# Seven block products in place of eight for 35 of 132 pairs of chunks in a decoder layer's feed-forward

## The chip, the cores and the metric

The kernel runs on one core of a Trainium2 chip. The metric is the device time of one execution in microseconds (us), lower is better. Engines are named as in the profile: PE (TensorE, matmuls), DVE (VectorE), ACT (ScalarE), POOL (GpSimd), SP (SyncE, here a queue that issues loads).

## What is computed

One decoder layer on 256 tokens of width 2048, in float32: two attention branches (gated DeltaNet and block-sparse attention), a gated merge, and a dense feed-forward. The change touches the last part:

```python
h = h + jnp.einsum('btd,de->bte', mix, w_out[l])
u = _rmsnorm(h, norm_ffn_w[l])
hid = jax.nn.silu(jnp.einsum('btd,df->btf', u, w_ffn_gate[l])) * jnp.einsum('btd,df->btf', u, w_ffn_up[l])
h = h + jnp.einsum('btf,fd->btd', hid, w_ffn_down[l])
```

The feed-forward is 5632 wide.

## The kernel before

Each matmul operand is split into a high part (float32r) and a remainder, and a product of two operands is three matmuls: high by high, high by remainder, remainder by high. Activations are split once and stay in SBUF (`uT`, the normalised input, and `hid`, the hidden layer, whose buffers are `low` and `high`). Weights stream from DRAM in 503 *units* of 128 x 1024 (512 KB), in the order of use. For each unit SP issues a load into `wraw` (7 buffers), ACT copies it to `whi` (L65), and DVE subtracts to `wlo` (L66); `whi` and `wlo` have 4 buffers each. I call the copy and the subtraction of one unit a *split*. `Weights.get` starts the splits of the next two units ahead; the fourth buffer is free only when PE has done with the unit four before.

A token-major job, `tm_job`, makes 512 output columns for both token tiles (n = 0, 1). One unit holds two *chunks* of 128 rows by 512 columns, so a unit is 2 chunks x 2 token tiles x 3 = 12 matmuls of 128 x 512 (L193 to L195), accumulating in 2 PSUM banks. The pool `mm` has two buffers of two banks each, the pool `aux` four of one bank. The feed-forward is 11 rounds c of a gate job and an up job, 8 units each. After a round, 8 transposes (L205) turn the 512 new hidden columns, and ACT and DVE split them (L860, L861). The down projection is 4 jobs j of 22 units; each ends with an addition of `h` on DVE and a store of the result. The last job finishes token tile 0 four chunks early.

Work beside the matmuls is queued in `late` and `chains`, and `tick()`, called after each unit, issues the next step. The tile framework orders the instructions of each engine; each engine then works through its own queue strictly in that order, so what waits at the head holds up all behind it.

Of the kernel before, what the change touches and what calls it, by code (L numbers as in the profile page):

```python
# [16 lines left out]
P = 128  # L17
# [19 lines left out]


class Weights:

    def __init__(self, nc, pool, src):
        self.nc, self.pool, self.src = nc, pool, src
        self.n = src.shape[0]
        self.raw, self.parts = {}, {}

    def load(self, u, f=slice(0, 1024)):
# [5 lines left out]

    def split(self, u, by_parts=False):
        if u in self.parts or u >= self.n:
            return
        self.load(u)
# [3 lines left out]
        self.parts[u] = (hi, lo)  # L62
# [7 lines left out]
        part(slice(0, 1024))  # L70

    def get(self, u):
        for k in range(u, u + RAW - 1):
            self.load(k)
        for k in range(u, u + SPLIT_AHEAD):
            self.split(k)
        return self.parts.pop(u)


@with_exitstack  # L80
def layer(ctx: ExitStack, tc: tile.TileContext, xT, xtok, params, consts, relt, w_bd, w, out):
# [91 lines left out]

    def tm_job(act, nk, last=0):

        get = act if callable(act) else lambda kc: act[:, kc]
        if last:
            ps = [aux.tile([P, 512], F32, name="ps", tag="aux") for _ in range(NT)]
        else:
            both = mm.tile([P, NT, 512], F32, name="ps", tag="mm")  # L180
            ps = [both[:, n] for n in range(NT)]
        order = [(kc, n) for kc in range(nk - last) for n in range(NT)]
        order += [(kc, n) for n in range(NT) for kc in range(nk - last, nk)]
        units = {}
        for kc, n in order:
            if kc // 2 not in units:
                units[kc // 2] = W.get(cursor[0])
                cursor[0] += 1
            hi, lo = units[kc // 2]
            sl = slice((kc % 2) * 512, (kc % 2) * 512 + 512)  # L190
            ah = get(kc)[:, n * P:(n + 1) * P]
            al = get(kc)[:, T + n * P:T + (n + 1) * P]
            nc.tensor.matmul(ps[n], ah, hi[:, sl], start=kc == 0, stop=False)  # L193
            nc.tensor.matmul(ps[n], ah, lo[:, sl], start=False, stop=False)  # L194
            nc.tensor.matmul(ps[n], al, hi[:, sl], start=False, stop=kc == nk - 1)  # L195
            if n == NT - 1 and kc % 2 == 1:
                tick()
        return ps

    def turn(src, evict):  # L200

        def steps():
            p = aux.tile([P, 4, P], F32, name="pT", tag="aux")
            for i in range(4):
                nc.tensor.transpose(p[:, i], src[:, i * P:(i + 1) * P], ident)  # L205
            evict(p)
        late.append(steps)

    ident = small("ident", [P])
    aT = acts.tile([P, KM, 512], F32R, name="aT", tag="actA")  # L210
    xrow = acts.tile([P, NT, DM], F32, name="xrow", tag="actB")
    with tc.tile_pool(name="xin", bufs=4) as xin:
# [17 lines left out]
        def x_part(k0):  # L230
            part = W.split(cursor[0], k0 == 0)
# [569 lines left out]
    for j in range(4):  # L801
        for n, m in gated(gates(), ybt(), "mixb", mdt):
            nc.vector.tensor_add(m, m, mix[j][n])
            turn(m, halved(j, n))


    h = acts.tile([P, NT, DM], F32, name="h", tag="actB")
    uT = acts.tile([P, KM, 512], F32R, name="uT", tag="actA")
    hss = small("hss", [NT, 4])

    def weighted(j, n):
        def evict(p):
            for i in range(4):
# [7 lines left out]
    for j in range(4):  # L821
# [35 lines left out]
    def parted(c, n):
        def evict(p):
            hi = hid(4 * c, 4)[:, :, n * P:(n + 1) * P]
            nc.scalar.copy(hi, p)  # L860
            nc.vector.tensor_sub(hid(4 * c, 4)[:, :, T + n * P:T + (n + 1) * P], p, hi.bitcast(F32))  # L861
        return evict

    for c in range(KF // 4):
        pg = tm_job(uT, KM)
        if c == 0:
            drain()
        gs = []
        for n in range(NT):
            g = fft("fg")  # L870
            nc.scalar.activation(g, pg[n], AF.Tanh, scale=r2h[:, n:n + 1])
            nc.vector.scalar_tensor_tensor(g, g, 1.0, pg[n], op0=ALU.add, op1=ALU.mult)
            gs.append(g)
        pu = tm_job(uT, KM)
        for n in range(NT):
            nc.vector.scalar_tensor_tensor(gs[n], pu[n], r2q[:, n:n + 1], gs[n], op0=ALU.mult, op1=ALU.mult)
            turn(gs[n], parted(c, n))
# [100 lines left out]
```

## Time and profile before

| | us |
|---|---|
| median of 3 runs (lowest, highest) | 1483.71 (1483.56, 1485.71) |
| the profiled execution's own time | 1483.21 |
| its span, first to last instruction | 1481.3 |
| PE busy in the span | 1473.0 |
| DVE busy | 867.4 |
| ACT busy | 677.8 |
| POOL busy | 31.8 |

Busy time of PE is the sum over matmuls whose ends are modelled; waits are read from the views of waits and of the timeline.

### The profile page before, as it was taken

Reading aid. Unit: us, or ns where it says so; the run is one execution under the profiler, and the core shown is the slowest. Engines: PE = TensorE matmul, PEld = TensorE weight load, DVE = VectorE, ACT = ScalarE, POOL = GpSimd, SP = SyncE. Lnnn points to the kernel's source line nnn. Section 1 sums busy time; section 2 is a strip of 40 time slices with the busy share of each in tenths; the row PEclk is TensorE's granted clock in tenths of the full one; section 3 lists DMA queues with packets and bytes.
Section 4 is the critical chain, followed back from the end, with each engine's and each line's share of the span. In section 5 each row is a group of like instructions: output and inputs, shape, how many; then the busy total and the mean of one; then the engine's idle time right before and its main releaser. Section 6 shows DMA issues by size and latency. Waiting matters only on the chain.

```text
span 1481.3 us, 18784 instructions
## 1 busy us (share of the span) xinstructions
PE 1473.0 (99%) x7182; PEld 1230.7 (83%) x7182; DVE 867.4 (59%) x1188; ACT 677.8 (46%) x968; POOL 31.8 (2%) x32
## 2 busy tenths in 40 slices
PE   9999999999999999999999999999999999999998
PEld 8888888888888888888888888888888888888887
DVE  6887689776764545555665554555554555444443
ACT  6554446645454444444554444443444443333332
POOL 0010000110000000000000000000000000000000
PEclk9999999999999999999999999999999999999999
DMA  9457545575456666677666666666666666676671
GB/s 376 161 179 195 158 142 174 163 188 164 150 164 181 192 195 188 183 220 220 185 186 188 193 189 193 187 187 190 192 189 193 186 187 190 193 211 204 195 209 61
DMA packets 77449, 277.81 MB, mean 188 GB/s; under 512 B 8752, under 2 KB 9392, under 8 KB 76976
## 3 DMA queue, kind: packets, MB, share of 16 engines
q1 hardware_dynamic: 75888, 272.03, 61.0%
q10 hardware_dynamic: 992, 3.02, 0.9%
q0 software_dynamic: 480, 1.57, 0.3%
q8 instruction: 56, 0.92, 0.2%
q14 instruction: 33, 0.27, 0.0%
HBM read 274.36 MB, written 2.23 MB: 187 GB/s over the span
## 4 chain that ended last, share of the span: by engine, by line
PE 97%; DVE 1%; issue 0%; DMA 0%; ACT 0%; POOL 0%; SPq 0%; DVEq 0%; ACTq 0%
PE ps L193 28%; PE ps L194 28%; PE ps L195 28%; PE ps L166 6%; PE ps L167 3%; PE pT L205 1%; PE pga L456 0%; DVE wlo L66 0%; DMA wraw<-in_w 0%; PE pb L300 0%; PE pX L541 0%; PE pY L534 0%; PE pU L584 0%; PE pO L592 0%; PE ptr L432 0%
## 5 line engine op out<-in xcount | busy, mean ns | idle before, releaser
L66 DVE TENSOR_TENSOR wlo<-wraw,whi 128x1024 fp32r<-128x1024 f32 (+1 forms) x505 | 617.5, 1225 | 507.4 <-ACT whi L65 506.7
L65 ACT CAST whi<-wraw 128x1024 fp32r<-128x1024 f32 (+1 forms) x505 | 530.2, 1051 | 709.3 <-PE ps L195 615.9
L193 PE MATMUL ps<-whi,uT 128*128 128x512 f32 x704 | 274.8, 390 | 0.0
L195 PE MATMUL ps<-whi,uT 128*128 128x512 f32 x704 | 273.9, 389 | 0.0
L194 PE MATMUL ps<-wlo,uT 128*128 128x512 f32 x704 | 273.9, 389 | 0.0
L193 PE MATMUL ps<-whi,aT 128*128 128x512 f32 x512 | 204.5, 399 | 0.0
L194 PE MATMUL ps<-wlo,aT 128*128 128x512 f32 x512 | 200.0, 391 | 0.1
L195 PE MATMUL ps<-whi,aT 128*128 128x512 f32 x512 | 199.8, 390 | 0.0
L195 PEld LDWEIGHTS ps<-whi,uT 128*128 128x128 f32 x704 | 132.2, 188 | 27.4
L194 PEld LDWEIGHTS ps<-wlo,uT 128*128 128x128 f32 x704 | 132.2, 188 | 27.1
L193 PEld LDWEIGHTS ps<-whi,uT 128*128 128x128 f32 x704 | 132.2, 188 | 27.0
L166 PE MATMUL ps<-aT,whi 128*128 128x512 f32 x384 | 136.9, 399 | 1.9 <-DVE aT L237 1.9
L195 PEld LDWEIGHTS ps<-whi,aT 128*128 128x128 f32 x512 | 96.1, 188 | 20.2
L193 PE MATMUL ps<-whi,high 128*128 128x512 f32 x288 | 112.0, 389 | 0.0
L194 PE MATMUL ps<-wlo,high 128*128 128x512 f32 x288 | 112.0, 389 | 0.0
L195 PE MATMUL ps<-whi,high 128*128 128x512 f32 x288 | 112.0, 389 | 0.0
L193 PEld LDWEIGHTS ps<-whi,aT 128*128 128x128 f32 x512 | 96.2, 188 | 18.8
L194 PEld LDWEIGHTS ps<-wlo,aT 128*128 128x128 f32 x512 | 96.3, 188 | 18.6 <-DVE wlo L66 0.4
L167 PE MATMUL ps<-aT,wlo 128*128 128x256 f32 x384 | 107.6, 280 | 0.9 <-DVE wlo L66 0.9
L166 PEld LDWEIGHTS ps<-aT,whi 128*128 128x128 f32 x384 | 72.1, 188 | 18.3 <-DVE aT L237 2.2
L167 PEld LDWEIGHTS ps<-aT,wlo 128*128 128x128 f32 x384 | 72.4, 189 | 1.6 <-DVE wlo L66 1.4
L193 PEld LDWEIGHTS ps<-whi,high 128*128 128x128 f32 x288 | 54.1, 188 | 11.3
(328 smaller groups left out, 1373.1 us busy)
## 6 DMA issues: line engine op xcount, KB each, us to landing
wraw<-in_w SPq DMA_DIRECT2D x503, 512.0 KB, 3.7
xrow<-in_xtok SPq DMA_DIRECT2D x1, 2048.0 KB, 13.6
lb<-dm ACTq DMA_DIRECT2D x2, 1024.0 KB
xr<-in_xtok SPq DMA_DIRECT2D x8, 256.0 KB, 5.3
xc<-in_xT SPq DMA_DIRECT2D x3, 512.0 KB, 7.3
out<-fo POOLq DMA_DIRECT2D x6, 256.0 KB, 3.8
bias<-in_relt SPq DMA_DIRECT2D x4, 256.0 KB, 3.9
xc<-in_xT ACTq DMA_DIRECT2D x2, 256.0 KB, 4.4
```

Source lines behind the costliest of these rows:

```text
L65: self.last_hi = self.nc.scalar.copy(hi[:, f], raw[:, f])
L66: self.last_lo = self.nc.vector.tensor_sub(lo[:, f], raw[:, f], hi[:, f].bitcast(F32))
L166: nc.tensor.matmul(ps[:, j], hi[:, sl], act[:, kc], start=kc == 0, stop=False)
L167: nc.tensor.matmul(ps[:, j, :T], lo[:, sl], act[:, kc, :T], start=False, stop=kc == nk - 1)
L193: nc.tensor.matmul(ps[n], ah, hi[:, sl], start=kc == 0, stop=False)
L194: nc.tensor.matmul(ps[n], ah, lo[:, sl], start=False, stop=False)
L195: nc.tensor.matmul(ps[n], al, hi[:, sl], start=False, stop=kc == nk - 1)
L205: nc.tensor.transpose(p[:, i], src[:, i * P:(i + 1) * P], ident)
```

## The change

Two 512-column jobs become one job of 1024 columns, `super_job`: gate and up of a round together, and two output blocks of the down projection. Its eight block products for a pair of chunks are (2 chunks of k) x (2 token tiles) x (2 halves of the columns). For 35 pairs (2 of 8 in each of the 11 rounds, 5 and 8 of 22 in the two down jobs; 132 pairs in all) these are replaced by seven products of sums of blocks. Four results of the seven pairs collect in the job's own banks (`ps`), and the others in four more banks (`pw`), which are put together once per job.

- **Splits.** A plain pair is two units, split whole. A pair of seven products has four splits: the left half of the first unit (`b11`), the second unit (`b2`), and both units again (`t`) after four subtractions in place on DVE (L96, L97, L99, L100). Its PE work per split is 3, 6, 6 and 6 matmuls.
- **Sums of activations.** `make_sums` forms four sums of blocks on POOL (one 128 x 512 addition and four of 128 x 128), copied on ACT and subtracted on DVE into `usum` (2, for all rounds) or `dsum` (8, for both down jobs). Its temporaries `fsum` have 2 buffers.
- **`after`.** When a job's last pair of seven is done, ACT copies the four `pw` banks into `ft`, and POOL makes four additions of 128 x 512 (eight in a down job, where it also adds `h`).
- **`swiglu`.** DVE adds the job's own banks to `ft`, then makes the gate product from SBUF; 8 transposes follow. Jobs alternate between `mm` and `aux` for `ps`, and the transposes and `pw` take the banks of the other pool, which held the previous job's results.
- **h in DRAM.** `h` is stored to DRAM by four DMAs of POOL's queue after the output projection and loaded again by four.

```diff
+FFN_PAIRS = (3, 5)
+FFN_ORDER = [[0, 1, 2, 4, 6, 3, 5, 7]] + [list(range(KM // 2))] * (DFF // 512 - 1)
+DOWN_PAIRS = (4, 8, 12, 15, 18, 2, 6, 10)
+DOWN_USED = [(4, 8, 12, 15, 18), DOWN_PAIRS]
...
+        left, right = slice(0, 512), slice(512, 1024)
+        part(left if kind == "b11" else slice(0, 1024))
+        if kind == "b11":
+            self.load(u + 1)
+            self.nc.vector.tensor_sub(raw[:, left], raw[:, right], raw[:, left])
+            self.nc.vector.tensor_sub(raw[:, right], self.raw[u + 1][:, left], raw[:, right])
+        if kind == "b2":
+            self.nc.vector.tensor_sub(raw[:, left], raw[:, left], self.raw[u - 1][:, left])
+            self.nc.vector.tensor_sub(raw[:, right], raw[:, right], raw[:, left])
...
+            if seven:
+                todo += [([(("s", 0), (2 * p, 0), 0)], 0),
+                         ([(("m", 1), (sums[p], 3), 0), (("m", 0), (2 * p + 1, 0), 1)], 1),
+                         ([(("s", 1), (sums[p], 0), 0), (("s", 3), (sums[p], 2), 1)], 0),
+                         ([(("s", 2), (sums[p], 1), 0), (("m", 2), (2 * p + 1, 1), 1)], 2)]
+            else:
+                todo += [([(("m", 2 * n + f), (2 * p, n), f) for n in range(NT) for f in range(2)], 1),
+                         ([(("m", 2 * n + 1 - f), (2 * p + 1, n), f) for n in range(NT) for f in range(2)], 1)]
...
+        if spare[0] == "mm":
+            both = mm.tile([P, NT, 512], F32, name="pT", tag="mm")
+            p = [both[:, n].rearrange("p (i t) -> p i t", i=4) for n in range(NT)]
+        else:
+            p = [aux.tile([P, 4, P], F32, name="pT", tag="aux") for _ in range(NT)]
...
+        nc.gpsimd.dma_start(hsave[:, :, fs], h[:, :, fs])
...
+    def make_sums(g, c):
...
+        f = fft("fsum", 2).rearrange("p (k t) -> p k t", k=2)
+        nc.gpsimd.tensor_add(f, c[:, :, :T], c[:, :, T:])
+        a11, a21, a12, a22 = f[:, 0, :P], f[:, 0, P:], f[:, 1, :P], f[:, 1, P:]
+        t = fft("fsum", 2).rearrange("p (k t) -> p k t", k=4)
+        nc.gpsimd.tensor_add(t[:, 0], a21, a22)
+        nc.gpsimd.tensor_sub(t[:, 1], t[:, 0], a11)
+        nc.gpsimd.tensor_sub(t[:, 2], a11, a21)
+        nc.gpsimd.tensor_sub(t[:, 3], a12, t[:, 1])
+        yield
+        nc.scalar.copy(g[:, 0], t)
+        nc.vector.tensor_sub(g[:, 1], t, g[:, 0].bitcast(F32))
+        yield
...
+        t = [fft("ft", 4) for _ in range(4)]
+        for a, b in zip(t, s):
+            nc.scalar.copy(a, b)
+        nc.gpsimd.tensor_add(t[2], t[0], t[2])
+        nc.gpsimd.tensor_add(t[3], t[2], t[3])
+        nc.gpsimd.tensor_add(t[2], t[2], t[1])
+        nc.gpsimd.tensor_add(t[1], t[3], t[1])
...
+    def down_sums():
+        for i, p in enumerate(DOWN_PAIRS):
+            yield from make_sums(dsum[:, i], hid(2 * p, 2))
```

Three places of the instruction order. First DVE in the first half of a round, from the end of a round's matmuls to the subtraction after the transposes (`fg` is the gate product, `pT` the transposed PSUM tile). Before:

```order
L66 TENSOR_TENSOR wlo<-wraw,whi 128x1024 x7
L876 SCALAR_TENSOR_TENSOR fg<-ps,r2q,fg 128x512 x2
L66 TENSOR_TENSOR wlo<-wraw,whi 128x1024 x2
L861 TENSOR_TENSOR low<-pT,low 128x4x128 x2
L66 TENSOR_TENSOR wlo<-wraw,whi 128x1024 x6
```

In the changed kernel, from the last step of `swiglu` through the first pair of seven of round 2:

```order
L88 TENSOR_TENSOR wlo<-wraw,whi 128x1024
L960 TENSOR_TENSOR low<-pT,low 128x4x128
L88 TENSOR_TENSOR wlo<-wraw,whi 128x1024
L960 TENSOR_TENSOR low<-pT,low 128x4x128
L88 TENSOR_TENSOR wlo<-wraw,whi 128x1024 x2
L88 TENSOR_TENSOR wlo<-wraw,whi 128x512
L96 TENSOR_TENSOR wraw<-wraw 128x512
L88 TENSOR_TENSOR wlo<-wraw,whi 128x1024
L97 TENSOR_TENSOR wraw<-wraw 128x512
L99 TENSOR_TENSOR wraw<-wraw 128x512
L100 TENSOR_TENSOR wraw<-wraw 128x512
L88 TENSOR_TENSOR wlo<-wraw,whi 128x1024 x8
```

The two subtractions behind the transposes now stand one behind each `t` split of pair 3 (the first two `L88` rows); the row of 128x512 opens pair 5. Second, PE in round 6, after the fifth unit, with buffer numbers (`pw` 8840 and 8841 are two-bank buffers of `mm`; `pT` 8801 holds the second of them until it is read out):

```order
L299 MATMUL pT_8801<-ident_80,fg_8716 128x128 x4
L283 MATMUL pw_8840<-whi_8783,uT_5835 128x512
...
L283 MATMUL pw_8840<-whi_8836,usum_6659 128x512
L284 MATMUL pw_8840<-wlo_8837,usum_6659 128x512
L285 MATMUL pw_8840<-whi_8836,usum_6659 128x512
L283 MATMUL pw_8841<-whi_8836,usum_6659 128x512
```

Before, all 8 transposes stood in a row; now in even rounds the second four stand after the sixth unit, directly ahead of the pair of seven. Third, DVE in the first down job around its first pair of seven (pair 4). Before, from the round's last subtraction to the end of down job 0:

```order
L861 TENSOR_TENSOR high<-pT,high 128x4x128 x2
L66 TENSOR_TENSOR wlo<-wraw,whi 128x1024 x20
L882 TENSOR_TENSOR fo<-ps,h 128x512 x2
```

In the changed kernel, from the third of the eight sums to the seventh:

```order
L976 TENSOR_TENSOR dsum<-fsum,dsum 128x512
L88 TENSOR_TENSOR wlo<-wraw,whi 128x512
L960 TENSOR_TENSOR high<-pT,high 128x4x128 x2
L96 TENSOR_TENSOR wraw<-wraw 128x512
L976 TENSOR_TENSOR dsum<-fsum,dsum 128x512
L97 TENSOR_TENSOR wraw<-wraw 128x512
L88 TENSOR_TENSOR wlo<-wraw,whi 128x1024
L976 TENSOR_TENSOR dsum<-fsum,dsum 128x512
L99 TENSOR_TENSOR wraw<-wraw 128x512
L100 TENSOR_TENSOR wraw<-wraw 128x512
L88 TENSOR_TENSOR wlo<-wraw,whi 128x1024
L976 TENSOR_TENSOR dsum<-fsum,dsum 128x512
```

All eight sums stand between the splits of units 5 to 15 of down job 0, three of them inside the splits of pair 4.

## Rows read from the trace of the kernel before

**Rows 1.** The page, part 1: busy time by engine; and TensorE's granted clock.
```profile
span 1481.3 us, 18784 instructions
PE 1473.0 (99%) x7182; PEld 1230.7 (83%) x7182; DVE 867.4 (59%) x1188; ACT 677.8 (46%) x968; POOL 31.8 (2%) x32
...
PEclk9999999999999999999999999999999999999999
```

**Rows 2.** The chain that ended last, by engine; then all waits of PE.
```profile
PE 97%; DVE 1%; issue 0%; DMA 0%; ACT 0%; POOL 0%; SPq 0%; DVEq 0%; ACTq 0%
...
PE ps L166 <- DVE aT L237: 1.9, 1, 1.9
PE busy L228 <- DVE ones L116: 1.1, 1, 1.1
PE ps L167 <- DVE wlo L66: 0.9, 1, 0.9
PE pb L300 <- DVE bw L297: 0.5, 1, 0.5
```

**Rows 3.** Timeline in round 5: start, us, engine, line, tile.
```profile
1001.38 0.39 PE L193 MATMUL ps<-whi,uT 128*128 128x512 f32 x1
1001.60 0.39 PE L194 MATMUL ps<-wlo,uT 128*128 128x512 f32 x1
1001.62 1.05 ACT L65 CAST whi<-wraw 128x1024 fp32r<-128x1024 f32 x1 [1.67 <-PE ps L195]
1001.83 0.39 PE L195 MATMUL ps<-whi,uT 128*128 128x512 f32 x1
1002.06 0.39 PE L193 MATMUL ps<-whi,uT 128*128 128x512 f32 x1
...
1002.71 1.23 DVE L66 TENSOR_TENSOR wlo<-wraw,whi 128x1024 fp32r<-128x1024 f32 x1 [1.49 <-ACT whi L65]
```

**Rows 4.** Windows: PE, PEld, DVE, ACT, POOL busy (x), clock, DMA share, GB/s.
```profile
795.80:840.20 44.40, 44.40 (x202) 36.86 (x201) 23.40 (x22) 19.00 (x20) 0.00 (x0) 1.00 0.65 190
```

**Rows 5.** Groups by line and form: DVE, then ACT (busy us, mean ns | idle before).
```profile
L66 DVE TENSOR_TENSOR wlo<-wraw,whi 128x1024 fp32r<-128x1024 f32 x503 | 616.1, 1227 | 502.5 <-ACT whi L65 501.7 <-PE pPT L733 0.6
L876 DVE SCALAR_TENSOR_TENSOR fg<-ps,r2q,fg 128x512 f32<-128x512 f32 x22 | 15.5, 746 | 4.5 <-PE ps L195 4.5
L828 DVE TENSOR_TENSOR h<-ps,xr 128x512 f32<-128x512 f32 x8 | 5.2, 686 | 1.6 <-PE ps L195 1.6
L803 DVE TENSOR_TENSOR mixb<-mixb,mix 128x512 f32<-128x512 f32 x8 | 5.1, 684 | 0.0
L65 ACT CAST whi<-wraw 128x1024 fp32r<-128x1024 f32 x503 | 529.0, 1053 | 707.1 <-PE ps L195 615.9 <-PE ps L166 35.5 <-issue 21.4
L860 ACT CAST high<-pT 128x512 fp32r<-128x512 f32 x18 | 9.6, 586 | 0.0
L65 ACT CAST whi<-wraw 128x512 fp32r<-128x512 f32 x2 | 1.2, 610 | 2.2 <-DMA wraw<-in_w 2.2
```

**Rows 6.** Groups of POOL by line and form.
```profile
L501 POOL TENSOR_TENSOR k<-k,kd 128x512 f32<-128x512 f32 x2 | 2.1, 1040 | 168.6 <-DVE erq L640 121.9 <-DVE bk L445 46.6
L969 POOL MEMSET const-uint8-127<- 128x1 uint8 x1 | 0.1, 103 | 0.0
```

**Rows 7.** Timeline of DVE and POOL, 107 to 112 us.
```profile
107.30 1.49 POOL L452 TENSOR_TENSOR mt<-dec,bk 128x512 f32<-128x512 f32 x1
107.81 2.06 DVE L66 TENSOR_TENSOR wlo<-wraw,whi 128x1024 fp32r<-128x1024 f32 x1
108.86 1.90 POOL L452 TENSOR_TENSOR dec<-dec,rk 128x512 f32<-128x512 f32 x1
...
110.73 1.29 POOL L484 TENSOR_TENSOR ct<-mt,cst 128x512 f32<-128x512 f32 x1
111.34 0.68 DVE L457 TENSOR_TENSOR mt<-mt,pga 128x512 f32<-128x512 f32 x1
```

**Rows 8.** What SP's queue waited for (us, times, longest), and landing of a weight load.
```profile
SPq L53 <- DVE wlo L66: 1071.1, 442, 13.1
...
wraw<-in_w SPq DMA_DIRECT2D x503, 512.0 KB, 3.7
```

**Rows 9.** Timeline at the end: last matmul, addition, store.
```profile
1477.07 0.39 PE L195 MATMUL ps<-whi,high 128*128 128x512 f32 x1
1477.49 0.69 DVE L882 TENSOR_TENSOR fo<-ps,h 128x512 f32<-128x512 f32 x1 [2.03 <-PE ps L195]
1478.22 0.34 ACTq L883 DMA_DIRECT2D out<-fo  x1
```

**Rows 10.** Durations of one subtraction-like line on DVE: min/median/max ns.
```profile
L466 DVE TENSOR_TENSOR mtmp<-mt,cst x4: 910/1344/1789, 107.0 to 301.6; 128x512 f32<-128x512 f32 x4
```

More of the change, by code (lines that the diff above doesn't have):

```diff
@@ L46, in __init__ @@
         self.raw, self.parts = {}, {}
+        jobs = _super_jobs()
+        self.first = self.n - 2 * sum(len(job) for job in jobs)
+        self.plan, self.at = [("all", u) for u in range(self.first)], 0
+        u = self.first
+        for seven in (f for job in jobs for _, f in job):
+            self.plan += [("b11", u), ("b2", u + 1), ("t", u), ("t", u + 1)] if seven else [("all", u), ("all", u + 1)]
+            u += 2
     def load(self, u, f=slice(0, 1024)):
@@ L172, in fm_job, with tm_job @@
         return fm_jobs(act, nk, 1)[0]
[L174 to L189, printed above, removed]
-            sl = slice((kc % 2) * 512, (kc % 2) * 512 + 512)
[L191 to L196, printed above, removed]
+    def tm_job(act, nk):
+        both = mm.tile([P, NT, 512], F32, name="ps", tag="mm")
+        ps = [both[:, n] for n in range(NT)]
+        for kc in range(nk):
+            if kc % 2 == 0:
+                hi, lo = W.get()
+            sl = slice((kc % 2) * 512, (kc % 2) * 512 + 512)
+            for n in range(NT):
+                ah = act[:, kc, n * P:(n + 1) * P]
+                al = act[:, kc, T + n * P:T + (n + 1) * P]
+                nc.tensor.matmul(ps[n], ah, hi[:, sl], start=kc == 0, stop=False)
+                nc.tensor.matmul(ps[n], ah, lo[:, sl], start=False, stop=False)
+                nc.tensor.matmul(ps[n], al, hi[:, sl], start=False, stop=kc == nk - 1)
+            if kc % 2 == 1:
@@ L862, in parted @@
         return evict
-    for c in range(KF // 4):
[L865 to L877, printed above, removed]
@@ new lines, in layer, with ffn_setup, after @@
+    usums = {}
+    def ffn_setup():
+        by_stage.close()
+        later["ff"] = ff = ctx.enter_context(tc.tile_pool(name="ff", bufs=1))
+        later["high"] = ff.tile([P, KF - H, 512], F32R, name="high")
+        yield
+        for p in FFN_PAIRS:
+            usums[p] = ff.tile([P, 2, 4, P], F32R, name="usum", tag="sum", bufs=2)
+            yield from make_sums(usums[p], uT[:, 2 * p:2 * p + 2])
+    parts = []
+    def after(s):
+        t = [fft("ft", 4) for _ in range(4)]
[5 more added lines that the diff above has]
+        nc.gpsimd.tensor_add(t[1], t[3], t[1])
+        parts.append([t[0], t[2], t[3], t[1]])
@@ new lines, in layer @@
+    jobs = _super_jobs()
+    kinds = ("aux", "mm")
+    chains.append(ffn_setup())
+    for c in range(KF // 4):
+        ps = super_job(kinds[c % 2], jobs[c], lambda kc: uT[:, kc], {p: lambda p=p: usums[p] for p in FFN_PAIRS}, after)
+        under_way.append(c)
+        chains.append(swiglu(c, ps, parts.pop()))
+    dsum = acts.tile([P, len(DOWN_PAIRS), 2, 4, P], F32R, name="dsum", tag="actA")
+    def down_sums():
+        for i, p in enumerate(DOWN_PAIRS):
+            yield from make_sums(dsum[:, i], hid(2 * p, 2))
@@ new lines, in down_end, with after_down @@
+    def down_end(j, ps, t, dmas):
+        for i in range(4):
+            n, f = divmod(i, 2)
+            nc.vector.tensor_add(t[i], t[i], ps[i])
+            dmas[i].dma_start(out[:, n, 512 * (2 * j + f):512 * (2 * j + f + 1)], t[i])
+            yield
+        if under_way:
+            under_way.pop()
+    chains.append(down_sums())
+    down = {p: lambda i=i: dsum[:, i] for i, p in enumerate(DOWN_PAIRS)}
+    for j in range(2):
+        hx = [later["ff"].tile([P, NT, 512], F32, name="hx", tag="sum", bufs=2) for _ in range(2)]
+        for f in range(2):
+            nc.gpsimd.dma_start(hx[f], hsave[:, :, 512 * (2 * j + f):512 * (2 * j + f + 1)])
+        def after_down(s):
+            after(s)
+            for i in range(4):
+                n, f = divmod(i, 2)
+                nc.gpsimd.tensor_add(parts[0][i], parts[0][i], hx[f][:, n])
+        ps = super_job(kinds[(KF // 4 + j) % 2], jobs[KF // 4 + j], hid, down, after_down, 2 * j)
+        if j == 0:
+            under_way.append(j)
+            chains.append(down_end(j, ps, parts.pop(), [nc.gpsimd] * 4))
@@ L886, in _bucket @@
+    for _ in down_end(1, ps, parts.pop(), [nc.sync, nc.scalar] * 2):
+        pass
 def _bucket():
```

163 lines of the change are left out of this document (121 added, 42 removed).

## The prediction

> **What bounds the kernel now.** I read the page's busy times and the chain of waits first. PE is busy 1473.0 of 1481.3 us, at a granted clock of 9 tenths or more in every slice [rows 1]; 97% of the chain that ended last is PE's, and all its waits together are 4.4 us, all early in the program [rows 2]. So every matmul taken away is worth its spacing, as long as the others still deliver. The timeline gives that spacing: L193 at 1001.38 and again at 1002.06 with three matmuls between, 0.227 us each; the 0.39 us of a row overlaps the next one's [rows 3]. A unit of 12 is then 2.72 us, and a round of 192 matmuls 43.5 us, with 8 transposes 44.4 us, which is the window of a whole round [rows 4]. In it DVE works 23.4 us and ACT 19.0: there is room, but how much of it lies where it is needed must be asked locally. The copy of a split starts 0.24 us after PE's matmul that opens a unit (1001.62 after 1001.38), since it waits for the `whi` buffer of four units before [rows 3]; then 1.05 us copy, 0.04 us, 1.23 us subtraction: 2.56 us, 5.6 us before PE wants it.
>
> **What is removed.** Each of the 35 pairs loses one block product of three matmuls: 105 x 0.227 = **-23.8 us**. The code and the order ahead of the feed-forward are the same but for names, so nothing moves there. A round becomes 186 matmuls and the transposes, 43.0 us.
>
> **What is added and lies beside PE.** Prices [rows 5]: split 1.053 on ACT and 1.227 on DVE, half a split 0.61 and about 0.69, a DVE operation of 512 from SBUF 0.684, with one input in PSUM 0.686, the scaled one 0.746, an ACT copy from PSUM 0.586. DVE in a round: 12 plain splits 14.7 us; two pairs of seven, each 3.5 splits and four subtractions, 4.3 + 2.7 = 7.0, together 14.1; `swiglu` and the reading of the transposes 7.0 us. That is 35.8 of 43.0 us. ACT: 25 us by the same sum. On average both fit. A pair of seven alone doesn't: 7.0 us of DVE in 21 x 0.227 = 4.76 us of PE, so it lives on the slack of the plain pair beside it (2.45 in 5.44 us), and with four buffers it can only run three splits ahead. The tightest is the second `t`: its copy may start when PE opens `b11`, 3 + 6 + 6 matmuls or 3.4 us ahead; the split takes 2.56 us, and PE wants the remainder only at the unit's second matmul. So 1.07 us are left if DVE is free at that moment. In the second down job plain and seven alternate: DVE 9.5 us in 10.2 us of PE, which holds by the same walk. I cost these at nothing; without that cover each 0.1 us is 3.5 us over 35 pairs.
>
> `after`: four copies (2.4 us of ACT) and four POOL additions at 1.04 us [rows 6] start some 10 us ahead of a round's end, and DVE has only plain splits there: nothing. The stores and loads of `h` add 4 MB to a DMA share of 0.65 [rows 4]: nothing. Weight loads wait for `wlo` of seven units before, 442 times [rows 8]; a pair of seven frees its buffers later, by two splits, but a load lands in 3.7 us [rows 8] and is wanted some 13 us after: nothing. The end keeps its shape, one addition and one store behind the last bank, where now 1477.07 leads to 1478.22 [rows 9].
>
> **What lands on the path.** Three places.
>
> First, round 0 takes its two pairs of seven one behind the other. Count from PE's start of the eighth unit: it opens the first `b11` at 8.2 us, and the second `t` of that pair is copied from 8.4 and subtracted by 10.7. Then DVE has half a split, a subtraction, a split, three subtractions and the next `t`: 0.69 + 0.69 + 1.23 + 2.05 + 1.23 = 5.9, done at 16.6; PE wants it at 15.0 + 0.2. **+1.4 us.**
>
> Second, in even rounds the second four transposes stand after the sixth unit, and `pT` holds the buffer that `pw`'s second half takes. From the round's start: fifth unit ends 13.6, four transposes 0.44, sixth unit to 16.8, transposes, `b11` at 17.2, `b2` 17.9, `t` 19.24; its second product, into that buffer, 19.92. The second `t` is copied 17.44 to 18.5, the transposed tile 18.5 to 19.1; DVE subtracts the `t` until 19.7 and then the tile until 20.4. PE waits 0.5 us, in rounds 2, 4, 6, 8 and 10: **+2.6 us.** In odd rounds all transposes come earlier and both readings are done by 18.3.
>
> Third, the eight sums of the first down job. A sum's four small POOL additions need the buffer that the sum before gives back only after its DVE subtraction, then comes ACT's copy, then DVE's subtraction, which stands at the head of DVE's queue between splits. A 128 x 128 addition on POOL is in no row. The nearest are 1.04 us for 512 columns and 0.10 for one column [rows 6], the bounds; I take 0.34, which is 0.10 and a quarter of the rest. A step is then 4 x 0.34 + 0.59 + 0.68 + 0.15 of handovers = 2.8 us. The first sum ends about 11.0 us after the job's start. If the engines run freely, the fourth ends at 19.6, the fifth at 22.3, and the first `t` of pair 4, behind two more subtractions, at 24.8, just when PE wants it (24.9); the sixth at 25.4 and the second `t` at 26.6, 0.4 us late. But POOL and DVE get in each other's way when both of DVE's inputs are in SBUF: a `wlo` that met a POOL multiplication took 2.06 us instead of 1.23, the next POOL one took 1.90 instead of 1.04, and a DVE operation from PSUM kept its 0.68 beside one [rows 7]. If each step's POOL work first lets pass the splits and subtractions that stand between the sums (1.2, 1.2, 1.3, 1.9 and 2.5 us up to the sixth), the second `t` comes 8 us later still, and the seventh sum adds one or two: 0.4 to 10.5 us. DVE often stands idle at a sum's wait, and POOL goes first then, so I take a value above the middle: **+6 us.**
>
> The Trainium skill, page "SBUF — State Buffer", section "Who interferes with whom", says that a DVE instruction with two SBUF inputs and a GpSimd instruction that reads SBUF share a port held for a whole instruction, so that the second to start is fully blocked, and that one SBUF input doesn't contend. The trace agrees, with the 2.06, 1.90 and 0.68 us above. By the rule alone the third term would be 10.5 us and the time 1473.9 us; without it 0.4 us and 1463.8 us.
>
> **Sum.** -23.8 + 1.4 + 2.6 + 6 = -13.8 us. Against the profiled execution's own 1483.2 us, which is 0.5 us under the median of the three runs, that gives 1469.4 us; I say **1469.4 us**.
>
> **Rivals.** (A) Everything is hidden. For it: PE waited for nothing after the first stage [rows 2], and my three places are built from handovers of a few tenths. Then 1483.2 - 23.8 = 1459.4, with the sums at 0.4 and the other two places as worked out 1463.8. (B) DVE is late in more places. DVE and POOL block each other fully in the sums, 10.5 us, and the cover of 1.07 us in a pair of seven is thin: if 17 of the 35 pairs lose 0.4 us more (6.8 us), 1.4 + 2.6 + 10.5 + 6.8 = 21.3 us come back, 1480.7; with a third of those pairs 1476. (C) Slower. The four subtractions in place cost what L466, a DVE operation of the same size, took beside POOL: 1.34 us, up to 1.79 [rows 10], against 0.68. Four times 0.66 is 2.6 us a pair, 1.07 covered, 1.6 us lost 35 times: 55 us, and 1469.4 + 55 = 1524 us. It decides against the change from 13.8 / 35 = 0.39 us a pair beyond the cover, so from 1.05 us a subtraction. Against it: L466 ran from 107.0 us on, in POOL's stretch [rows 7, 10], POOL is idle where these stand, and L803 with both inputs in SBUF took 0.684 [rows 5]. (D) No change to within 0.2%, or 3 us, which is about what a measurement of this kernel can tell: were POOL's small additions at their upper bound of 1.04 us, the five steps up to the sixth sum would grow by 2.8 us each, 14 us, and 1469.4 would become 1483.4.
>
> **Chances.** The sum's own case, 1463.8 to 1476 us: 0.53. (A) 0.20. (B) 0.18. (D) 0.04. (C) 0.05. Faster by over 0.2% is the first three, 0.91; within 0.2% 0.04; slower 0.05. The range goes from (A)'s better half to (B)'s end: 1460 to 1480 us leaves out the lowest of (A) and all of (C) and (D), under 2 in 10.
>
> **What the profile will show.** PE: 105 fewer matmuls of 512 and still 0.227 us apart. Round 0: a wait of PE for `wlo` of about 1.4 us ahead of the second pair of seven's first `t`. Even rounds: waits of about 0.5 us for DVE's reading of `pT`, none in odd ones. Down job 0: several us of waits for `wlo` between its units 9 and 13, DVE in turn waiting for ACT's `dsum`, ACT for POOL. Down job 1: none. DVE near 36 us in a round of 43. The prediction is wrong low if PE waits in every pair of seven, and wrong high if down job 0 runs through its sums without a gap, or if POOL's small additions take about 0.1 us.

## The result, and the profile after

The changed kernel takes 1473.88 us, the median of 4 runs (1473.38 to 1475.54), against 1483.68 us for the kernel before beside it (4 runs): 0.9933 of the time, 95% interval 0.9915 to 0.9950. That is 9.8 us less, where 14.3 was forecast; 1473.88 lies inside the range of 1460 to 1480 us.

The page of the changed kernel, first the busy times, then PE's share and granted clock in 40 slices of 36.8 us:

```profile
PE 1458.2 (99%) x7077; PEld 1213.5 (82%) x7077; DVE 1078.7 (73%) x1452; ACT 759.9 (52%) x1100; POOL 200.9 (14%) x148
...
PE   9999999999999999999999999999999999899998
...
PEclk9999999999999999999999999999999999899999
```

PE was without a dent before [rows 1]; now its 35th slice has an 8 and the granted clock has one there too. DVE has 211 us more to do in all [rows 1]. The view of PE's waits, whose total was 4.4 us before [rows 2]:

```profile
PE pw L284 <- DVE wlo L88: 3.3, 2, 2.6
...
PE ps L284 <- DVE wlo L88: 1.6, 2, 1.2
PE pw L283 <- ACT whi L87: 1.4, 1, 1.4
...
PE ps L283 <- ACT whi L87: 0.7, 1, 0.7
```

These four rows, all in the changed part, are 7.0 us of waits for splits. 0.7 of it lies in round 0 and 0.4 near the end; the other 5.9 lie in 16 us of down job 0, whose windows show what came with them (busy time and matmuls in brackets of PE, weight loads, DVE, ACT, POOL, then granted clock):

```profile
1227.08:1250.44 23.36, 23.36 (x108) 19.41 (x107) 17.49 (x22) 11.19 (x15) 12.07 (x16) 1.00 0.50 150
1250.44:1266.10 15.66, 9.71 (x24) 6.13 (x23) 10.20 (x10) 5.58 (x8) 13.63 (x15) 0.67 0.29 84
1266.10:1350.00 83.90, 83.90 (x372) 69.45 (x371) 61.76 (x60) 43.30 (x48) 14.00 (x9) 1.00 0.65 209
```

In the middle one PE is busy for 9.71 us only, and at a granted clock of 0.67; ahead of it and behind it PE is busy throughout, at 1.00. PE there, in its timeline (start, duration, idle time before it):

```profile
1250.44 0.39 PE L283 MATMUL ps<-whi,dsum 128*128 128x512 f32 x1
1252.05 0.50 PE L284 MATMUL ps<-wlo,dsum 128*128 128x512 f32 x1 [1.21 <-DVE wlo L88]
...
1253.08 0.40 PE L285 MATMUL ps<-whi,high 128*128 128x512 f32 x1
1254.91 0.51 PE L283 MATMUL pw<-whi,dsum 128*128 128x512 f32 x1 [1.44 <-ACT whi L87]
1258.07 0.80 PE L284 MATMUL pw<-wlo,dsum 128*128 128x512 f32 x1 [2.65 <-DVE wlo L88]
1258.66 0.63 PE L285 MATMUL pw<-whi,dsum 128*128 128x512 f32 x1
1259.08 0.63 PE L283 MATMUL pw<-whi,dsum 128*128 128x512 f32 x1
...
1260.51 0.80 PE L283 MATMUL pw<-whi,dsum 128*128 128x512 f32 x1
1261.95 0.80 PE L284 MATMUL pw<-wlo,dsum 128*128 128x512 f32 x1 [0.65 <-DVE wlo L88]
...
1265.95 0.39 PE L284 MATMUL ps<-wlo,high 128*128 128x512 f32 x1
```

Twenty-two steps lead from 1250.44 to 1265.95, 15.51 us where 22 x 0.227 = 4.99 would do: 10.5 us are lost. Four steps are too long by 1.38, 1.60, 2.93 and 1.21 us, together 7.1. The other 3.4 us are in steps between and behind them, nearly all from 1258.07 to 1265.95, where most matmuls start 0.42 to 0.43 us apart: the 1.2 GHz level, where 0.227 us is the 2.4 GHz one. The Trainium skill, page "TensorE: Matmul & The Clock Gate", section "Back-to-back issue gap", gives 512 columns divided by 1.2 GHz for it, 0.427 us, and the rows agree.

These slow steps are not 3.4 us of a loss of their own. Behind the last of the four waits (1261.95) PE goes on without a wait until it needs the next remainder that stands behind a sum in DVE's queue, that of the unit after the next:

```profile
1265.24 1.23 DVE L976 TENSOR_TENSOR dsum<-fsum,dsum 128x512 fp32r<-128x512 f32 x1 [1.95 <-ACT dsum L975]
1266.40 1.21 DVE L88 TENSOR_TENSOR wlo<-wraw,whi 128x1024 fp32r<-128x1024 f32 x1
...
1268.04 0.39 PE L284 MATMUL ps<-wlo,high 128*128 128x512 f32 x1
```

It is ready at 1267.61, and PE comes for it at 1268.04. At 0.227 us a step the nine steps up to 1265.95 would have taken 2.0 us less, and PE would have come at 1266.1 and waited; and the slow steps ahead of 1261.95 only shortened the wait that ended there. By these rows the lower clock cost some 0.4 us here (an estimate, which takes it that the row of sums doesn't hang on PE's pace), and the row of sums the rest.

What PE waits for there is the row of sums. One step of it, in the timeline of POOL, ACT and DVE:

```profile
1234.99 0.69 DVE L976 TENSOR_TENSOR dsum<-fsum,dsum 128x512 fp32r<-128x512 f32 x1
...
1235.82 0.46 POOL L970 TENSOR_TENSOR fsum<-fsum 128x128 f32<-128x128 f32 x1 [10.01 <-DVE dsum L976]
...
1236.57 1.22 DVE L88 TENSOR_TENSOR wlo<-wraw,whi 128x1024 fp32r<-128x1024 f32 x1 [0.89 <-ACT whi L87]
1236.67 1.45 POOL L971 TENSOR_TENSOR fsum<-fsum 128x128 f32<-128x128 f32 x1
1238.19 0.46 POOL L973 TENSOR_TENSOR fsum<-fsum 128x128 f32<-128x128 f32 x1
1238.69 0.62 ACT L975 CAST dsum<-fsum 128x512 fp32r<-128x512 f32 x1 [2.15 <-POOL fsum L973]
1238.73 1.30 POOL L967 TENSOR_TENSOR fsum<-high 128x512 f32<-128x512 f32 x1
...
1239.34 1.24 DVE L976 TENSOR_TENSOR dsum<-fsum,dsum 128x512 fp32r<-128x512 f32 x1 [1.55 <-ACT dsum L975]
```

A 128 x 128 addition takes POOL 0.46 us, and 1.45 when a `wlo` runs. ACT stands idle at the head of its queue for 2.15 us and DVE for 1.55, each with splits behind that could run. The first sum ends at 1235.68, the sixth at 1260.77: 5.0 us a step in the mean, where 2.8 was forecast for free engines.

The program up to the feed-forward is the same in all kernels here, but its length differs from execution to execution: PE's first matmul on `uT` starts at 748.50 us in the profile of before, at 751.07 in this one, and between 748.3 and 752.1 in the others. So below I compare, beside the medians, the **stretch**: from that matmul's start to the start of the last one. It is 1477.07 - 748.50 = 728.57 us before and 1469.62 - 751.07 = 718.55 us after, 10.0 less. With the 23.8 us removed and nothing lost it would be 704.8, so 13.8 us came back.

### The profile page after: what moved, and what is told of

Read it like the earlier page. It is cut to its first block, busy times and chain, and to the rows that moved or that the text cites. A ratio compares the mean times of both kernels' runs of the same rounds, so it can differ in the third digit from the quotient of the medians.

```text
span 1473.8 us, 19231 instructions
## 1 busy us (share of the span) xinstructions
PE 1458.2 (99%) x7077; PEld 1213.5 (82%) x7077; DVE 1078.7 (73%) x1452; ACT 759.9 (52%) x1100; POOL 200.9 (14%) x148
## 4 chain that ended last, share of the span: by engine, by line
PE 93%; DVE 3%; ACT 1%; issue 1%; POOL 1%; DMA 0%; SPq 0%; DVEq 0%; POOLq 0%; ACTq 0%
PE ps L283 13%; PE ps L284 13%; PE ps L285 13%; PE ps L218 11%; PE ps L219 11%; PE ps L220 11%; PE ps L199 6%; PE ps L200 3%; PE pw L284 2%; PE pw L285 2%; PE pw L283 2%; PE pT L299 1%; DVE wlo L88 1%; ACT whi L87 1%; DVE dsum L976 0%
## 5 line engine op out<-in xcount | busy, mean ns | idle before, releaser
L88 DVE TENSOR_TENSOR wlo<-wraw,whi 128x1024 fp32r<-128x1024 f32 (+1 forms) x575 | 702.8, 1236 | 282.1 <-ACT whi L87 277.0
L87 ACT CAST whi<-wraw 128x1024 fp32r<-128x1024 f32 (+1 forms) x575 | 585.3, 1025 | 604.2 <-PE ps L285 233.6
L283 PE MATMUL ps<-whi,uT 128*128 128x512 f32 x572 | 223.8, 391 | 0.7 <-ACT whi L87 0.7
L285 PE MATMUL ps<-whi,uT 128*128 128x512 f32 x572 | 222.8, 390 | 0.0
L284 PE MATMUL ps<-wlo,uT 128*128 128x512 f32 x572 | 222.8, 389 | 0.0
L283 PEld LDWEIGHTS ps<-whi,uT 128*128 128x128 f32 x572 | 107.4, 188 | 23.0 <-ACT whi L87 1.1
L285 PEld LDWEIGHTS ps<-whi,uT 128*128 128x128 f32 x572 | 107.4, 188 | 22.6
L284 PEld LDWEIGHTS ps<-wlo,uT 128*128 128x128 f32 x572 | 107.4, 188 | 21.9
L219 PEld LDWEIGHTS ps<-wlo,aT 128*128 128x128 f32 x512 | 96.3, 188 | 18.5 <-DVE wlo L88 0.4
L199 PEld LDWEIGHTS ps<-aT,whi 128*128 128x128 f32 x384 | 73.5, 192 | 18.5 <-DVE aT L333 2.0
L284 PE MATMUL ps<-wlo,high 128*128 128x512 f32 x216 | 84.7, 392 | 0.4 <-DVE wlo L88 0.4
L283 PE MATMUL ps<-whi,high 128*128 128x512 f32 x216 | 84.6, 392 | 0.0
L285 PE MATMUL ps<-whi,high 128*128 128x512 f32 x216 | 84.6, 392 | 0.0
L997 POOL TENSOR_TENSOR ft<-ft 128x512 f32<-128x512 f32 x13 | 23.5, 1805 | 446.7 <-ACT ft L996 446.7
## 6 DMA issues: line engine op xcount, KB each, us to landing
xrow<-in_xtok SPq DMA_DIRECT2D x1, 2048.0 KB, 13.7
```

Source lines behind the costliest of these rows:

```text
L283: nc.tensor.matmul(ps, ah, hi[:, sl], start=i == use[0], stop=False)
L284: nc.tensor.matmul(ps, ah, lo[:, sl], start=False, stop=False)
L285: nc.tensor.matmul(ps, al, hi[:, sl], start=False, stop=i == use[-1])
L997: nc.gpsimd.tensor_add(t[2], t[0], t[2])
```

## Experiments

My theory: what comes back is mainly the packed row of eight sums in down job 0. Its steps are long, and they stand at the head of ACT's and DVE's queues, so that the splits behind them come late; the rest of the change costs a microsecond here and there. The main rival: the pairs of seven themselves are more than DVE and ACT can feed, sums or not.

**Sums spread out.** Each half of a down sum is held back behind one more split.

```diff
         for i, p in enumerate(DOWN_PAIRS):
-            yield from make_sums(dsum[:, i], hid(2 * p, 2))
+            steps = make_sums(dsum[:, i], hid(2 * p, 2))
+            for _ in range(2):
+                with tc.issue_after(W.last_hi.ins), tc.issue_after(W.last_lo.ins):
+                    next(steps)
+                yield
+            yield from rest(2)
```

> Only the place of the eight down sums in the queues changes: each step of a sum stands behind a split's copy and subtraction of its own, so that the sums spread over more units of down job 0. My theory is that the 10.6 us lost in the changed kernel at 1250 to 1266 us are the chain of sums packed at the head of DVE's and ACT's queues (7.1 us of waits) and the lower clock that follows the waits (3.5 us). Then both go, at most 1 us stays, and the median falls from 1473.9 to 1463.5 to 1464.5. Rival 1, the pairs of seven of down job 0 are themselves more than DVE and ACT can do, whatever stands between them: the waits stay at 6 us or more, 1470 to 1474. Rival 2, the clock falls in that stretch for a reason of its own: the waits go and the 3.5 us stay, about 1467.

Measured: 1464.37 us (1463.78 to 1465.11), 0.9864 of before (0.9851 to 0.9878); the stretch is 1458.07 - 750.11 = 707.96 us, 10.6 less than the changed kernel. Two of its sums in the timeline, and the window around them:

```profile
1254.66 0.68 DVE L976 TENSOR_TENSOR dsum<-fsum,dsum 128x512 fp32r<-128x512 f32 x1
...
1255.48 1.31 POOL L970 TENSOR_TENSOR fsum<-fsum 128x128 f32<-128x128 f32 x1 [6.49 <-DVE dsum L976]
...
1257.72 1.37 POOL L973 TENSOR_TENSOR fsum<-fsum 128x128 f32<-128x128 f32 x1
...
1262.43 0.61 ACT L975 CAST dsum<-fsum 128x512 fp32r<-128x512 f32 x1
...
1263.17 0.69 DVE L976 TENSOR_TENSOR dsum<-fsum,dsum 128x512 fp32r<-128x512 f32 x1
```

```profile
1250.00:1266.00 16.00, 16.00 (x72) 13.24 (x71) 11.97 (x14) 8.92 (x11) 6.83 (x8) 1.00 0.76 263
```

POOL is as slow as in the changed kernel, with 1.31 and 1.37 us beside a `wlo`, and this step, the shortest of them, is 8.5 us long. But ACT and DVE come to a sum only when it is ready, with no idle time ahead of L975 and L976, and PE is busy without a gap at a clock of 1.00. So the place in the queues alone makes or removes the whole 10.6 us, and the lower clock with it, and both rivals fall: the pairs of seven of down job 0 are the same ones.

**Sums made on DVE.** The places stay; the steps get short.

```diff
-        nc.gpsimd.tensor_add(f, c[:, :, :T], c[:, :, T:])
+        eng = nc.vector if len(usums) == len(FFN_PAIRS) else nc.gpsimd
+        eng.tensor_add(f, c[:, :, :T], c[:, :, T:])
...
-        nc.gpsimd.tensor_add(t[:, 0], a21, a22)
+        eng.tensor_add(t[:, 0], a21, a22)
```

(and the three subtractions likewise)

> The five additions of each down sum are made on DVE in place of POOL. No POOL instruction stands beside DVE in down job 0 then, and two handovers between engines go, but DVE has eight times one addition of 512 (0.68 us) and four of 128 x 128 (estimate 0.2 us each, between the 0.10 us of a one-column POOL row and the 0.68), 12 us more in all. If the exclusion of POOL and DVE made the stall, a step is 0.7 + 0.8 + 0.6 + 0.75 + 0.2, about 3 us in place of 4.7, and the stall shrinks to 3 to 5 us with the clock staying up: 1466 to 1469. If it is the work at the head of DVE's queue that makes it, DVE's 12 us more leave the stall at 10 us or lengthen it: 1474 to 1480.

Measured: 1463.21 us (1462.49 to 1464.84), 0.9858 (0.9844 to 0.9871); stretch 1457.13 - 749.18 = 707.95 us. A sum in DVE's timeline:

```profile
1233.13 0.69 DVE L977 TENSOR_TENSOR dsum<-fsum,dsum 128x512 fp32r<-128x512 f32 x1
1233.85 0.29 DVE L971 TENSOR_TENSOR fsum<-fsum 128x128 f32<-128x128 f32 x1
1234.06 0.28 DVE L973 TENSOR_TENSOR fsum<-fsum 128x128 f32<-128x128 f32 x1
```

The windows of the same kernel:

```profile
1225.22:1250.00 24.78, 24.78 (x115) 20.62 (x114) 24.53 (x43) 14.23 (x18) 0.00 (x0) 1.00 0.50 153
1250.00:1266.00 16.00, 16.00 (x72) 13.24 (x71) 15.76 (x27) 8.74 (x11) 0.00 (x0) 1.00 0.72 252
```

Better than I expected: nothing is left of the stall, where I had left 3 to 5 us. The four small additions start 0.2 us apart, and of a sum's steps only the copy on ACT leaves DVE. DVE works for 24.5 of 24.8 us, and PE runs through: a busy DVE is no harm here, one that stands still at its queue's head is. Short steps and free heads, the two ways out of the stall, come to the same stretch within 0.01 us.

**Other buffers for a sum's first addition.** If a step were long because it waits for the buffer of the one before, this would shorten it.

```diff
-        f = fft("fsum", 2).rearrange("p (k t) -> p k t", k=2)
+        f = fft("fg" if len(usums) == len(FFN_PAIRS) else "fsum", 2).rearrange("p (k t) -> p k t", k=2)
```

> The first addition of a down sum goes into another pair of buffers (those of the gate product, idle there), so it and the four small additions no longer share two buffers. Theory (a sum waits for the one before it to give back its buffer): the first addition, 0.5 to 1.3 us with its handover, leaves a step of 4.7 us; over the six sums up to the stalled pair some 4 to 6 us of the 10.6 come back, 1468 to 1470. Rival (the steps are long because POOL and DVE exclude each other, and the instructions stand in the same places): the stall is the same within 1 us, 1473 to 1475.

Measured: 1483.20 us (1481.96 to 1485.16), 0.9991 (0.9983 to 1.0000), and a stretch of 1478.01 - 750.88 = 727.13 us, 8.6 more than the changed kernel. Both sides missed, through a mistake of mine, which POOL's and PE's timeline show (the last row is a window, with the columns of the windows above):

```profile
1241.18 2.98 POOL L967 TENSOR_TENSOR fg<-high 128x512 f32<-128x512 f32 x2 [15.55 <-PE pT L299]
...
1260.31 0.80 PE L283 MATMUL pw<-whi,dsum 128*128 128x512 f32 x1 [5.63 <-ACT whi L87]
...
1250.77:1265.58 14.81, 4.95 (x11) 2.64 (x11) 8.98 (x8) 2.80 (x4) 14.34 (x17) 0.61 0.12 29
```

`fg` isn't idle: it holds the gate product until the last transpose has read it, so the first sums start at 1241.18, when the changed kernel has done its second (1240.58). The sixth sum ends at 1272.36 in place of 1260.77, 11.6 us later, and PE loses 8.6 us more. Two things follow. The row's due time is what counts: three quarters of the delay of the sums reach PE. And other buffers don't shorten the row: from the second sum (1250.77) to the fifth (1265.58) a step still is 4.9 us. But it is another step, since POOL now goes from sum to sum with hardly a pause, busy for 14.34 of 14.81 us, and its own five additions set the pace. So the run doesn't show what share the buffers had in a step of the changed kernel.

**Pairs of seven of round 0 apart.**

```diff
-FFN_ORDER = [[0, 1, 2, 4, 6, 3, 5, 7]] + [list(range(KM // 2))] * (DFF // 512 - 1)
+FFN_ORDER = [[0, 1, 2, 4, 3, 6, 5, 7]] + [list(range(KM // 2))] * (DFF // 512 - 1)
```

> Round 0 takes a plain pair between its two pairs of seven (order 0 1 2 4 3 6 5 7 in place of 0 1 2 4 6 3 5 7). Theory: its 1.15 us of waits at 786 to 787 us go, nothing else changes, 1473.9 becomes 1472.7. Rival: the first pair of seven then comes two units earlier, before its sums of uT are ready or while DVE still has the sums to do, and PE waits there as long or longer: 1473.9 or more.

Measured: 1474.72 us (1473.54 to 1478.03), 0.9934 (0.9920 to 0.9947), and a stretch of 1472.12 - 752.08 = 720.04 us, 1.5 more than the changed kernel: nothing gained. 0.6 of it lies in round 0 and 0.9 in down job 0, where the steps of the 1.2 GHz level go on until 1269.6 us, 17.6 us after the first wait where it was 15.5. In the changed kernel PE waited in round 0, in the second pair of seven, where a matmul of the second `t` needs a copy that waits for the last subtraction (L100):

```profile
786.52 2.00 ACT L87 CAST whi<-wraw 128x1024 fp32r<-128x1024 f32 x2 [0.39 <-DVE wraw L100]
787.62 0.50 PE L283 MATMUL ps<-whi,uT 128*128 128x512 f32 x1 [0.71 <-ACT whi L87]
```

With the pairs apart the rival holds, at the first pair:

```profile
772.05 0.69 DVE L976 TENSOR_TENSOR usum<-fsum,usum 128x512 fp32r<-128x512 f32 x1 [1.70 <-ACT usum L975]
...
778.71 0.50 PE L284 MATMUL pw<-wlo,usum 128*128 128x512 f32 x1 [0.93 <-DVE wlo L88]
```

The second sum of `uT`, which POOL makes, holds DVE until 772.7 us, 20.7 us after the start of the stretch, with the pair's splits behind it. It is the pattern of down job 0 in small.

**The down jobs plain.** Undoes one part: no pairs of seven, no sums, no combination there.

```diff
-DOWN_PAIRS = (4, 8, 12, 15, 18, 2, 6, 10)
-DOWN_USED = [(4, 8, 12, 15, 18), DOWN_PAIRS]
+DOWN_PAIRS = ()
+DOWN_USED = [(), ()]
...
-    chains.append(down_sums())
...
-            chains.append(down_end(j, ps, parts.pop(), [nc.gpsimd] * 4))
+            chains.append(down_end(j, ps, t, [nc.gpsimd] * 4))
```

(`t` are slices of the loaded `hx`, which here has the buffer of `dsum`)

> The down jobs are plain: no pairs of seven there, no down sums, no combination of banks at their ends; the feed-forward rounds keep their 22 pairs. 13 pairs times three matmuls come back, 39 x 0.227 = +8.8 us. Theory: what was lost in the changed kernel's down jobs belongs to the eight sums (10.6 us at 1250 to 1266 us) and to the combination at the end (0.8 us at 1460 us), so PE runs both down jobs without a gap: 1473.9 + 8.8 - 10.6 - 0.8 = 1471.3, faster than the changed kernel by 2.6 although it does more. Rival 1, wide jobs stall at their seam with the last round whether or not there are sums: PE still waits there and the time is above 1475, up to 1482.7. Rival 2, the stall of 1250 to 1266 also holds a debt from the rounds (DVE late from the pairs of seven): PE waits early in down job 0, 1473 to 1477.

Measured: 1472.37 us (1471.33 to 1473.14), 0.9919 (0.9905 to 0.9934); stretch 1467.29 - 750.91 = 716.38 us. With 39 matmuls more it is 2.2 us shorter than the changed kernel, against 2.6 expected, and the first 33 us of down job 0 have PE busy throughout:

```profile
1227.02:1260.00 32.98, 32.98 (x151) 27.43 (x150) 19.84 (x22) 14.86 (x16) 2.91 (x4) 1.00 0.80 262
```

So the wide jobs don't stall at their seam with the last round, and the rounds leave no debt. The down jobs' part of the change cost more than it saved.

**All ten sums on DVE, and round 0 apart.** The edit of the sums without its condition, and the order of above.

```diff
-        nc.gpsimd.tensor_add(f, c[:, :, :T], c[:, :, T:])
+        nc.vector.tensor_add(f, c[:, :, :T], c[:, :, T:])
...
-FFN_ORDER = [[0, 1, 2, 4, 6, 3, 5, 7]] + [list(range(KM // 2))] * (DFF // 512 - 1)
+FFN_ORDER = [[0, 1, 2, 4, 3, 6, 5, 7]] + [list(range(KM // 2))] * (DFF // 512 - 1)
```

> All ten sums, the two of round 0 as well, are made on DVE in place of POOL, and round 0 takes its pairs of seven apart (0 1 2 4 3 6 5 7). With the sums on POOL that order only moved round 0's wait (0.3 + 1.1 us at 776 to 779), since the second sum was ready at 772.7 us with its subtraction ahead of the first pair's splits. Theory: made on DVE, a sum takes about 0.7 + 4 x 0.28 us without turns between POOL and DVE, is out of the way some 3 to 4 us earlier, and round 0's wait goes: 1463.2 (down sums on DVE alone) becomes 1462.0. Rival: the ten extra DVE operations stand in DVE's queue among the splits of round 0 and PE waits for wlo as long as before: 1463 to 1464.

Measured: 1462.65 us (1461.54 to 1463.65), 0.9854 (0.9839 to 0.9869); stretch 1457.27 - 750.45 = 706.82 us, 1.13 less than with the down sums alone. PE's first pair of seven has no wait, and the expected 1.2 us are there, which the order by itself had not given. DVE's timeline:

```profile
766.90 0.68 DVE L88 TENSOR_TENSOR wlo<-wraw,whi 128x512 fp32r<-128x512 f32 x1
...
770.65 0.68 DVE L976 TENSOR_TENSOR usum<-fsum,usum 128x512 fp32r<-128x512 f32 x1
```

The time came out, but not for the reason I gave. Counted from the start of the stretch, the second sum of `uT` is done at 20.9 us, no sooner than with POOL (20.7), where I had said 3 to 4 us earlier. What moved is what stands behind it: the pair's first split starts at 16.5 us in place of 20.6, since two splits and two subtractions of the pair now come ahead of that sum's last step.

**The last combination on DVE.** The down sums on DVE, and the eight additions of `after` in down job 1.

```diff
-    def after(s):
+    def after(s, eng=nc.gpsimd):
...
-            after(s)
+            after(s, nc.vector if j else nc.gpsimd)
...
-                nc.gpsimd.tensor_add(parts[0][i], parts[0][i], hx[f][:, n])
+                (nc.vector if j else nc.gpsimd).tensor_add(parts[0][i], parts[0][i], hx[f][:, n])
```

> Down sums on DVE, and the eight additions of the last combination (down job 1) on DVE too. Theory: the 0.76 us that PE loses at 1460 us come from wlo and POOL's additions excluding each other (wlo 1.7 us and more, the additions 1.8 to 2.3); on DVE the eight take 8 x 0.68 = 5.5 us among plain splits that leave 2.45 us free in 5.44, so the wait goes: 1463.2 becomes 1462.4 to 1462.6. Rival: 5.5 us in one piece ahead of the last splits make PE wait longer than the 0.76 us: 1463.5 to 1465.

In the changed kernel, the timeline of the place:

```profile
1457.87 2.28 POOL L1057 TENSOR_TENSOR ft<-ft,hx 128x512 f32<-128x512 f32 x1
1459.50 1.73 DVE L88 TENSOR_TENSOR wlo<-wraw,whi 128x1024 fp32r<-128x1024 f32 x1 [0.51 <-ACT whi L87]
1461.28 0.50 PE L284 MATMUL ps<-wlo,high 128*128 128x512 f32 x1 [0.42 <-DVE wlo L88]
```

Measured: 1463.52 us (1461.39 to 1465.38), 0.9855 (0.9839 to 0.9872). The median doesn't tell this from 1463.21. The stretch is 1459.53 - 751.88 = 707.65 us, 0.30 less than with the down sums alone. The two long steps of PE at this place take 0.46 and 0.34 us in place of 0.81 and 0.34, so half of the loss is gone, and 0.35 us of it stay.

**All of it together.** The last two edits in one kernel.

```diff
+        nc.vector.tensor_add(f, c[:, :, :T], c[:, :, T:])
...
+FFN_ORDER = [[0, 1, 2, 4, 3, 6, 5, 7]] + [list(range(KM // 2))] * (DFF // 512 - 1)
...
+            after(s, nc.vector if j else nc.gpsimd)
```

> All sums and the last combination on DVE, and round 0 in the order 0 1 2 4 3 6 5 7: the two edits before together. Theory: both gains add up, 1463.2 - 1.2 - 0.7 = 1461.3 us, with only the even rounds' waits for the reading of the transposes (0.2 us a round) left of the 14 us. Rival: 0.3 to 1 us of each comes back as DVE waits, 1462 to 1464.

Measured: 1460.84 us (1460.38 to 1464.56), 0.9848 of before (0.9833 to 0.9862); stretch 1454.80 - 748.31 = 706.49 us, 12.1 less than the changed kernel and 1.7 above nothing lost. The longest of the waits of its PE, which like all of them in that view lies ahead of the feed-forward:

```profile
PE ps L199 <- DVE aT L333: 1.9, 1, 1.9
```

## Why the prediction was right, and where it was off

- **What is removed** (-23.8): right. Matmuls still start 0.227 us apart, 105 fewer; with every added wait taken out 22.1 of the 23.8 us are there (728.57 - 706.49).
- **Pairs of seven cost nothing in themselves**: right. No pair of the rounds 1 to 10 or of down job 1 makes PE wait, and with the sums out of the way none in down job 0. The subtractions in place took 0.69 us (L96 to L100).
- **First term, round 0** (+1.4): right in place and about in size; the step is 1.15 us too long, and taking it away gave 1.13. The wait was forecast for the first `t`'s remainder and came at the second one's copy, both held by the same row of DVE work. And one thing was missing: to put the pairs apart helps only where the first pair's splits don't stand behind the second sum in DVE's queue (16.5 in place of 20.6 us).
- **Second term, even rounds** (+2.6): wrong, about nothing at its place. The timeline of round 2 (below) shows why: the step that failed is "The second `t` is copied 17.44 to 18.5, the transposed tile 18.5 to 19.1". ACT copied the tile first (856.53), DVE had read it at 858.49, and PE took the bank at 858.60 with a step of 0.28 us for 0.227: 0.05 us in place of 0.5. Against 704.8 us, the last version keeps 1.7: 0.35 at the end of down job 1, the others in steps too long by under 0.12 us, spread over rounds and jobs, which I have not assigned one by one.
- **Third term, the eight sums** (+6): right in place and mechanism, wrong in size: 10.6 us, the upper end of 0.4 to 10.5. The step that failed is the choice between these two, "DVE often stands idle at a sum's wait, and POOL goes first then". From the end of the first sum (1235.68) to that of the sixth (1260.77) five steps take 25.1 us, where five of 2.8 are 14.0. Of the 11.1 us more, 8.3 are instructions of the sums that took longer while the other engine worked: 5.6 on POOL's small additions (as L971 above, 1.45 in place of 0.46, beside a `wlo`) and 5 x 0.54 on the `dsum` subtraction, which each time met the next sum's first addition (L967). The walk in which POOL lets all pass had 8.1 us for this. POOL's small addition at 0.46 us in place of the 0.34 I took makes 2.4 more, and the first sum was done 8.6 us after the job's start where I had 11.0. The two nearly cancel: the sixth sum is done at 33.7 us, where that walk says 25.4 + 8.1 = 33.5, and PE has the second `t` 8.6 us late, where it says 8.4. I had no term for the clock, and by the estimate above one of 0.4 us was due.
- **The rule of the Trainium skill's page "SBUF — State Buffer"**, section "Who interferes with whom": the third term by the rule alone, 10.5 us, is what was measured. That POOL and DVE exclude each other agrees with the rows (0.46 against 1.45 us, 0.69 against 1.24). That the whole time by the rule alone, 1473.9 us, is the measured one is luck in part: its sum holds 2.6 us for the second term that are not there and lacks 2.0 us of small steps that are. And the exclusion is no sufficient cause, as the spread sums show, where POOL is blocked as much and PE loses nothing.
- **The rivals**: (A)'s 1463.8 us is nearly what the spread sums gave (1464.37), but not what the change itself does. (B) came nearer in time than the sum did: its first half, the sums with full blocking at 10.5 us, came true, and its second did not, since no pair of seven lost its cover. (D) and (C) had no ground, at 0.46 us for POOL's small additions and 0.69 for the subtractions.
- **Not foreseen**: 0.7 us at the end, where `after` had been costed at nothing; additions on DVE took back 0.3 of it.

The timeline of ACT, DVE and PE for the second term:

```profile
856.53 0.58 ACT L959 CAST low<-pT 128x512 fp32r<-128x512 f32 x1
...
857.80 0.69 DVE L960 TENSOR_TENSOR low<-pT,low 128x512 fp32r<-128x512 f32 x1
...
858.60 0.44 PE L283 MATMUL pw<-whi,usum 128*128 128x512 f32 x1
858.88 0.40 PE L284 MATMUL pw<-wlo,usum 128*128 128x512 f32 x1
```

The terms of the prediction gave 1.4 + 2.6 + 6 = 10.0 us back; the runs took 1.1 + 0.3 + 10.6 away again and left 1.7 in small steps, 13.7 of the 13.8 us of the stretches. How the excess of a step's length divides is read from the durations in the changed kernel's trace; no run removed the exclusion and left the handovers.

## What to carry to other kernels

When a chain of small steps over several engines is put between regular work, look first at what stands behind its waiting instructions in each queue: the same eight sums cost 10.6 us where ACT and DVE waited at their heads, and nothing where they came to them ready, though each took longer. Work that looks free to a half-idle engine can be dearer than the same work on the busy one: the sums cost nothing on DVE, at 24.5 of 24.8 us busy, since only one step left the engine. And where the granted clock falls inside a stall, ask what PE would have met at full speed before the slow steps are counted as a loss: here 3.4 us of them cost, by the estimate above, some 0.4, because PE would have stood before the same row of sums.

## What the runs showed of the hardware

- In the changed kernel TensorE's granted clock fell to the 1.2 GHz level at 1255.7 us, when PE had lost 1.4 and 1.6 us in two steps and the third wait, of 2.9 us, had just begun; it came back at 1265.95. With the same four waits in the run with round 0 apart it fell at 1255.9, in the second wait, and came back at 1269.6 us, 17.6 us after the first wait in place of 15.5. With other buffers it fell at 1254.1, after a single wait of 2.4 us, and came back at 1274.6. Single waits of about 1 us (round 0, 787 us) left it at 0.227 us a step. So where the clock falls and comes back isn't fixed by the program. What it costs depends on what PE would have met: in the run with round 0 apart, where the level outlasted the stall, down job 0 lost 0.9 us more.
- A 128 x 128 addition takes POOL 0.46 us (0.42 from start to start) and DVE 0.28 us (0.2 from start to start); a 128 x 512 one takes about 1.3 us on POOL in down job 0, beside DVE's work, and 0.68 us on DVE.
- The part of the program ahead of the feed-forward, the same in every kernel, ended anywhere from 748.3 to 752.1 us, which is more than the differences between several of the versions; the medians alone would not have told them apart.
